# A two-block transformer forward pass: the last retention pair's norm kept on chip, scales stored as rows, and the stream's norm moved into attention

## The chip, the cores and the metric

The kernel runs on one core of one Trainium2 chip. The metric is the device time of one execution in microseconds (us). The engines are PE (matrix products), DVE (VectorE), ACT (ScalarE), POOL (GpSimd) and SP (which issues the DMAs); each executes its own queue in order.

## What is computed

The input is a sequence of 1024 tokens with 1024 channels, in float32. A first block of two hybrid layers (convolutions and windowed attention) is followed by a second block of two layers, each with differential attention and retention side by side, and then a gated FFN. Between the blocks stands an RMS norm. Of the second block, what matters here is:

```python
x = first_block(...)                       # ends in rmsnorm(x, final_norm_g)
for l in range(2):
    u = rmsnorm_2(h, attn_norm[l])
    rq, rk, rv, rg, dq, dk, dv = split(u @ w_in[l])
    ret = rmsnorm_2(retention(rq, rk, rv), ret_norm[l])   # 4 heads, norm over 128
    ret = silu(rg) * ret
    dif = rmsnorm_2(diff_attention(dq, dk, dv, lam), diff_norm[l]) * (1 - lam_init)
    h = h + concat([ret, dif]) @ w_out[l]
    u = rmsnorm_2(h, ffn_norm[l])
    h = h + (silu(u @ w_gate[l]) * (u @ w_up[l])) @ w_down[l]
return rmsnorm_2(h, final_norm)
```

## The kernel before, in words

Everything lies with channels on the 128 partitions and tokens along the free axis, in halves of 512 columns. A float32 product is made of three matmuls on operands split into a rounded high part and a rest (`split`, L189 and L190): high by high, high by low, low by high (L222, L224, L225 in `dense`). Weights are loaded by `load_w` (L202 on SP), their high part is cast on ACT (L205) and the rest is made on POOL (L194).

`second(l, last)` is one layer of the second block. It runs four heads of differential attention (`diff`), then two pairs of retention heads (`retention`, c = 0 and 1), while the projections of the next head and the gates are worked in between. Each finished group of query columns (256 in `diff`, 512 in `retention`) goes through `headnorm`: ACT copies it out of PSUM (L874), SP stores it to DRAM (L875), ACT squares it (L877). One group later, `put_off` has PE sum the columns (`colsum`, L258; DVE L261 takes the mean), POOL takes the power -1/2 (`rsq`, L267) and SP stores the scales to DRAM (L881), one element per descriptor, since tokens lie on the partitions there. The last group of a layer is done by `last_headnorm` (L888).

Later `normed_op` makes an operand of each head: `fetch` loads the head back (L898) and its row of scales, spread over all partitions (L899); DVE multiplies the two and the gain (L1036); for a retention head POOL multiplies the gate (L1038), which was spilled by `gate_spill` and is loaded in halves (L1034); then `split` (L189, L190). In layer 0 the residual stream `xd` still lacks the norm between the blocks: it is loaded (L1070), scaled by a gain on ACT (L1075) and multiplied with the row `R1` (L1064) on POOL (L1077).

The output projection is in two parts. `dense` takes the four differential heads' operands and adds the result to the stream (L1082); this is worked in between the retention of the second pair. `dense_half` takes the four retention heads' operands, for all eight output tiles of the first 512 tokens and then for the other 512 (L1135, L1137, L1138 in `block`), and its result (L1100) feeds the FFN.

The order of all instructions on each queue is planned when the kernel is built: the program is traced, earlier traced work has the higher priority, and an instruction may be put ahead of earlier work that isn't ready in the plan. Buffers come from pools with fixed counts (`xp` has 13 of 8 KB per partition, `dp` six of 2 KB, PSUM's `pt` two banks). `issue_after` keeps a store behind a given one in SP's queue.

The broadcast of a row of scales from tokens on partitions to all partitions is `bcast`: two DVE casts (L275, L276), and per 128 tokens two matmuls on an identity (L282).

Of the kernel before, what the change touches and what calls it, by code (L numbers as in the profile page):

```python
# [20 lines left out]
AF = mybir.ActivationFunctionType  # L21
ALU = mybir.AluOpType
AX = mybir.AxisListType

P = 128
S = 1024
D = 1024
KC = D // P
HW = 512
NT = S // P  # L30
# [28 lines left out]
C_FN1 = C_SINK + 8  # L59
C_AN2 = C_FN1 + 8  # L60
C_RN = C_AN2 + 16
# [4 lines left out]


NTAP0, NTAP = 3, 2
NGATE = 4
RM = 2  # L70
CPW = 256

# [1 line left out]
class Builder:  # L74
    def __init__(self, nc, tc, a, es):
        self.nc, self.tc, self.a, self.es = nc, tc, a, es
        self.n = 0
        self.pools = {}
        self.put_off = None
        self.ready, self.use_ready = [], False  # L80
        self.open(es, cp=1, rp=1, wp=3, xp=13, dp=6, sp=8)
        self.open(es, bass.MemoryType.PSUM, pa=3, ps=2, pt=2, po=1)
        self.open(es, bass.MemoryType.DRAM, dr=2)
# [781 lines left out]
            nc.scalar.copy(c, ps)  # L865
            nc.sync.dma_start(self.R1[:, t], c)

    def headnorm(self, O, n, y, t):

        nc = self.nc
        o = self.tl("ho", (P, HW))
        nc.scalar.copy(o[:, :n], O[:, :n])  # L874
        stored = nc.sync.dma_start(y[0][:, t], o[:, :n])  # L875
        q = self.tl("hq", (P, HW))
        nc.scalar.activation(q[:, :n], o[:, :n], AF.Square)  # L877
        if self.put_off is not None:
            r, rd = self.put_off()
            with self.tc.issue_after(stored.ins):  # L880
                nc.sync.dma_start(rd, r)  # L881
        self.put_off = lambda: (self.rsq(self.colsum([q[:, :n]], P)),
                                y[1][t.start // P:t.stop // P, :].rearrange("c p -> p c"))

    def last_headnorm(self):
        r, rd = self.put_off()
        self.put_off = None
        self.nc.sync.dma_start(rd, r)  # L888

    def nspill(self):  # L890

        return self.yspill(), self.tl("dr", (NT, P), tag="r", bufs=8)

    def fetch(self, y):

# [6 lines left out]
    def ret_units(self, w, c):  # L902
        return [self.proj(w, u) for u in (c, 2 + c, 4 + 2 * c, 5 + 2 * c)]

    def retention(self, l, c, units):
        nc = self.nc
        ys = []
        qf, kf = units[:2]
        ops = self.halves(kf, qf)
        Vs = [self.v_wide(units[2 + j]) for j in range(2)]  # L910
        for j in range(2):
            h = 2 * c + j
            V = Vs[j]
            dec = self.tl("tb", (P, S))
            nc.sync.dma_start(dec, self.a["c_dec"][h])
            y = self.nspill()
            for g in range(2):
                O = self.psT() if g else self.psO()
                nk = 4 * g + 4
                for kt in range(nk):  # L920
                    q0 = max(kt * P, g * HW)
                    n = (g + 1) * HW - q0
                    ps = self.psS()
                    self.scores(ps[:, :n], ops, j, slice(kt * P, kt * P + P), slice(q0, q0 + n))
                    p = self.tl("p", (P, HW))
                    nc.vector.tensor_tensor(p[:, :n], ps[:, :n],
                                            dec[:, q0 - kt * P:q0 - kt * P + n], ALU.mult)
                    pt = self.tl("tp", (P, HW), F32R), self.tl("tp", (P, HW), F32R)
                    nc.scalar.copy(pt[0][:, :n], p[:, :n])
                    if kt % RM:  # L930
                        nc.vector.tensor_tensor(pt[1][:, :n], p[:, :n], pt[0][:, :n].bitcast(F32),
                                                ALU.subtract)
                    else:
                        self.rest(pt[1][:, :n], p[:, :n], pt[0][:, :n])
                    for i, (lhsT, part) in enumerate(V(kt)):
                        nc.tensor.matmul(O[:, HW - n:HW], lhsT, pt[part][:, :n],
                                         start=(kt == 0 and i == 0),
                                         stop=(kt == nk - 1 and i == 2), skip_group_check=True)
                self.headnorm(O, HW, y, slice(g * HW, (g + 1) * HW))
            ys.append(y)  # L940
        return ys

# [3 lines left out]
    def diff(self, l, h, units):  # L946
# [54 lines left out]
            self.headnorm(O, 256, y, slice(g * 256, (g + 1) * 256))  # L1001
        return y

    def gate_spill(self, w, u):
        g = self.tl("dr", (P, S), tag="gate", bufs=4)

        def ev(t, ps):
            self.nc.sync.dma_start(g[:, t], self.silu2(ps, t))

        self.dense(w[u], self.x, ev)  # L1010
        return g
# [30 lines left out]
    def second(self, l, last):  # L1042
        import contextlib
        nc, a = self.nc, self.a
        w, wo = a["w_in_2"][l], a["w_out_2"][l]
        with contextlib.ExitStack() as es:
            self.open(es, pj=4, p=7, tp=6, kl=1, tb=2, ho=2, hq=3)
            self.open_klo()
            yd, gates = [], []
            units = self.diff_units(w, 0)  # L1050
            for h in range(4):
                yd.append(self.diff(l, h, units))
                units = self.diff_units(w, h + 1) if h < 3 else self.ret_units(w, 0)
                if h < NGATE:
                    gates.append(self.gate_spill(w, 8 + h))
            yr = self.retention(l, 0, units)
            units = self.ret_units(w, 1)
            yr += self.retention(l, 1, units)
            gates += [self.gate_spill(w, 8 + h) for h in range(NGATE, 4)]
            self.last_headnorm()  # L1060
            R1 = None
            if l == 0:
                R1 = self.tl("xp", (P, S))
                nc.sync.dma_start(R1, self.R1)  # L1064
            ops = [self.normed_op(yd[h], self.gdn[:, l:l + 1], self.xg) for h in range(4)]
            xs = []
            for d in range(0, KC, 2):
                two = self.tl("xp", (P, 2, S))
                for i in range(2):
                    nc.sync.dma_start(two[:, i, :], self.xd[d + i])  # L1070
                    xs.append(two[:, i, :])
            if l == 0:
                for d in range(KC):
                    for t in (slice(0, HW), slice(HW, S)):
                        nc.scalar.activation(xs[d][:, t], xs[d][:, t], AF.Copy,  # L1075
                                             scale=self.col(C_FN1 + d))
                        nc.gpsimd.tensor_tensor(xs[d][:, t], xs[d][:, t], R1[:, t], ALU.mult)  # L1077
            for d in range(KC):
                xr = xs[d]

                def ev(t, ps):
                    nc.vector.tensor_tensor(xr[:, t], ps, xr[:, t], ALU.add)  # L1082

                self.dense(wo[d][:, 0:4, :], ops, ev)
            ops = [self.normed_op(yr[h], self.col(C_RN + l), self.opt, gates[h]) for h in range(4)]
            es.close()
            self.open(es, fx=6, sw=SW, p1=LEAD)
            xd = [self.tl("dr", (P, S), tag=f"x{d}") for d in range(KC)]
            R = self.R = self.tl("rp", (P, S), tag="R")
            X, q, s1 = {}, [], [None, None]  # L1090
            full = slice(0, HW)
            scale = lambda h: self.row_scale(R, slice(h * HW, (h + 1) * HW), s1[h])
            for h in range(2):
                t = slice(h * HW, (h + 1) * HW)
                s1[h] = self.d2()
                for d in range(KC):
                    xr = xs[d]

                    def ev(t, ps):
                        nc.vector.tensor_tensor(xr[:, t], ps, xr[:, t], ALU.add)  # L1100
                        nc.sync.dma_start(xd[d][:, t], xr[:, t])
                        self.addsq(s1[h], full, xr[:, t], d == 0, eng=1)
                        nc.scalar.activation(xr[:, t], xr[:, t], AF.Copy,
                                             scale=self.col(C_FFN + 8 * l + d))

                    self.dense_half(wo[d][:, 4:8, :], ops, t, ev)
                    self.early_blocks(X, xs, q, h, d)
                    if h == 1 and d == 3:
                        scale(0)
            self.xd = xd  # L1110
            hd, ahead = self.ffn_hidden(a["w_gate_2"][l], a["w_up_2"][l], X,
                                        lambda: scale(1), self.late_blocks(X, xs))
            es.close()
            self.open(es, hx=7, wr=2, sw=1)
            self.ffn_out(l, hd, last, ahead)
# [615 lines left out]
```

## Time and profile before

| what | value |
|---|---|
| median of 3 runs (lowest to highest) | 3629.62 us (3627.13 to 3630.72) |
| the profiled execution's own time | 3628.38 us |
| its span, first to last instruction | 3626.6 us |
| PE busy | 3379.9 us, 93% |
| DVE, ACT, POOL busy | 2509.6, 1565.7, 2096.2 us |
| mean granted PE clock | 0.974 |

Times inside the span are counted from its start. Attention of layer 0 of the second block lies at about 1080 to 1420 us, its hand-over to the FFN at 1420 to 1565; layer 1's hand-over lies at 2700 to 2828. A wait is idle time of an engine just before an instruction, put down to what ended it ("<-"). PEld is PE's weight load, which overlaps the matmuls.

### The profile page before, as it was taken

The numbers are of one execution on the slowest core, as the hardware profiler recorded it, in microseconds if no ns is written. First come the engines' busy times: TensorE is split into PE (matmuls) and PEld (weight loads), VectorE is DVE, ScalarE is ACT, GpSimd is POOL, SyncE is SP. The second block draws the span as 40 slices with busy tenths as digits, with TensorE's granted clock in tenths as the row PEclk, the third lists the DMA queues.
The fourth block names the chain that finished last, engine by engine and source line by source line (L and its number), as shares of the span: only waits on it lengthen the run. The fifth ranks groups of instructions, "written<-read, shape, count | busy, mean of one in ns | idle before, by whom it ended". The sixth has DMA issues, their size and how long they took to land.

```text
span 3626.6 us, 46124 instructions
## 1 busy us (share of the span) xinstructions
PE 3379.9 (93%) x15872; PEld 2777.8 (77%) x15872; DVE 2509.6 (69%) x3947; ACT 1565.7 (43%) x3175; POOL 2096.2 (58%) x1859
## 2 busy tenths in 40 slices
PE   8999999899999999869999989999998789998897
PEld 6788888788888888657777767888886677777676
DVE  6756656655656765667776799766656677767997
ACT  4475442674444553353333333445443533333333
POOL 4785453984472334646666778623334566666784
PEclk9999999999999999989999999999998999999999
DMA  4112532122432335542111243323355422112432
GB/s 129 39 57 54 180 112 74 35 59 82 161 108 53 51 57 111 141 135 89 70 70 72 86 146 111 104 55 53 52 98 148 142 81 79 70 70 82 151 99 82
DMA packets 181451, 330.39 MB, mean 91 GB/s; under 512 B 48992, under 2 KB 59616, under 8 KB 181216
## 3 DMA queue, kind: packets, MB, share of 16 engines
q1 hardware_dynamic: 181216, 327.44, 31.8%
q8 instruction: 125, 2.05, 0.3%
q14 instruction: 110, 0.90, 0.1%
HBM read 250.23 MB, written 73.99 MB: 89 GB/s over the span
## 4 chain that ended last, share of the span: by engine, by line
PE 48%; DVE 10%; DMA 5%; POOL 3%; issue 3%; ACT 1%; SPq 0%; DVEq 0%; POOLq 0%; ACTq 0%
PE pa L222 5%; PE pa L225 5%; PE pa L224 5%; PE pa L1135 3%; PE pa L1137 3%; PE pa L1138 3%; PE T L1138 3%; PE T L1135 2%; PE T L1137 2%; PE ps L1135 2%; PE ps L1138 2%; PE ps L1137 2%; PE po L427 2%; DVE xp L1360 1%; PE ps L334 1%
## 5 line engine op out<-in xcount | busy, mean ns | idle before, releaser
L224 PE MATMUL pa<-xp,whi 128*128 128x512 f32 x2048 | 815.8, 398 | 10.7 <-DVE xp L190 10.7
L222 PE MATMUL pa<-xp,whi 128*128 128x512 f32 x2048 | 813.2, 398 | 11.8 <-ACT xp L189 8.3
L225 PE MATMUL pa<-xp,wlo 128*128 128x512 f32 x2048 | 814.4, 398 | 1.2 <-POOL wlo L194 1.2
L194 POOL TENSOR_TENSOR wlo<-raw,whi 128x512 fp32r<-128x512 f32 x304 | 432.2, 1423 | 468.0 <-ACT whi L205 445.8
L194 POOL TENSOR_TENSOR wlo<-xp,whi 128x512 fp32r<-128x512 f32 x248 | 360.3, 1456 | 192.3 <-ACT whi L1211 191.8
L224 PEld LDWEIGHTS pa<-xp,whi 128*128 128x128 f32 x2048 | 390.1, 190 | 89.9 <-DVE xp L190 16.1
L222 PEld LDWEIGHTS pa<-xp,whi 128*128 128x128 f32 x2048 | 389.8, 191 | 88.1 <-ACT xp L189 9.0
L225 PEld LDWEIGHTS pa<-xp,wlo 128*128 128x128 f32 x2048 | 390.3, 191 | 76.3 <-POOL wlo L194 2.0
L1135 PE MATMUL pa<-xp,whi 128*128 128x512 f32 x672 | 271.3, 405 | 66.8 <-ACT xp L189 22.3
L1211 ACT CAST whi<-xp 128x512 fp32r<-128x512 f32 x248 | 153.8, 620 | 408.1 <-PE T L1137 139.0
L205 ACT CAST whi<-raw 128x512 fp32r<-128x512 f32 x304 | 187.0, 615 | 267.6 <-PE pa L224 145.5
L446 POOL TENSOR_SCALAR p<-p,st 128x256 f32<-128x256 f32 (+4 forms) x224 | 158.1, 714 | 242.9 <-DVE st L985 120.8
L1138 PE MATMUL pa<-xp,wlo 128*128 128x512 f32 x672 | 265.5, 398 | 3.0 <-POOL wlo L194 2.9
L1137 PE MATMUL pa<-xp,whi 128*128 128x512 f32 x672 | 267.2, 398 | 0.0
L701 POOL TENSOR_TENSOR cc<-cc,prod 128x256 f32<-128x256 f32 x240 | 201.0, 859 | 30.0 <-ACT prod L700 23.8
L1135 PEld LDWEIGHTS pa<-xp,whi 128*128 128x128 f32 x672 | 129.0, 192 | 108.1 <-ACT xp L189 22.7
L420 DVE TENSOR_TENSOR tp<-T,tp 128x512 fp32r<-128x512 f32 (+2 forms) x224 | 131.4, 599 | 73.5 <-ACT tp L419 71.7
L980 ACT ACTIVATE p<-p,st 128x384 f32<-128x384 f32 (+3 forms) x192 | 117.1, 611 | 126.4 <-DVE st L973 125.8
L427 PE MATMUL po<-tp,xp 128*128 128x256 f32 (+1 forms) x1024 | 163.6, 279 | 5.1 <-ACT tp L419 4.8
L427 PEld LDWEIGHTS po<-tp,xp 128*128 128x128 f32 x1024 | 148.5, 189 | 24.3 <-ACT tp L419 8.7
L700 ACT ACTIVATE prod<-cc,c 128x256 f32<-128x256 f32 x240 | 119.0, 507 | 109.0 <-POOL cc L701 97.5
L1230 POOL TENSOR_TENSOR xp<-xp,R 128x512 f32<-128x512 f32 x80 | 111.1, 1389 | 84.5 <-DVE xp L1229 84.5
(316 smaller groups left out, 8129.2 us busy)
## 6 DMA issues: line engine op xcount, KB each, us to landing
raw<-w_in SPq DMA_DIRECT2D x208, 256.0 KB, 2.8
xp<-x SPq DMA_DIRECT2D x48, 512.0 KB, 7.3
xp<-w_gate SPq DMA_DIRECT2D x44, 512.0 KB, 5.4
xp<-w_up SPq DMA_DIRECT2D x44, 512.0 KB, 5.2
raw<-w_out SPq DMA_DIRECT2D x80, 256.0 KB, 3.1
x<-xp SPq DMA_DIRECT2D x80, 256.0 KB, 2.1
h<-xp SPq DMA_DIRECT2D x40, 512.0 KB, 3.0
xp<-h SPq DMA_DIRECT2D x80, 256.0 KB, 4.5
```

The costliest lines, as they stand in the source:

```text
L194: self.last_rest = self.nc.gpsimd.tensor_tensor(lo, src, hi.bitcast(F32), ALU.subtract)
L205: nc.scalar.copy(hi, raw)
L222: nc.tensor.matmul(ps[h], hi[:, k - k0, :], x[:, 0, t], start=(k == 0), stop=False)
L224: nc.tensor.matmul(ps[h], hi[:, k - k0, :], x[:, 1, t], start=False, stop=False)
L225: nc.tensor.matmul(ps[h], lo[:, k - k0, :], x[:, 0, t], start=False, stop=(k == nk - 1))
L427: nc.tensor.matmul(O[:, qs[0] * P:qs[0] * P + w], lhsT, pt[part][:, o:o + w], start=((kt, qs) == blocks[0] and i == 0), stop=((kt, qs) == ...
L446: self.nc.gpsimd.tensor_scalar(out, src, colm, 1.0, ALU.mult, ALU.mult)
L701: nc.gpsimd.tensor_tensor(acc[:, i:i + CPW], acc[:, i:i + CPW], q, ALU.add)
L1135: nc.tensor.matmul(ps, hi[:, k, :], xh, start=(start and k == 0), stop=False, skip_group_check=True)
L1137: nc.tensor.matmul(ps, hi[:, k, :], xl, start=False, stop=False, skip_group_check=True)
L1138: nc.tensor.matmul(ps, lo[:, k, :], xh, start=False, stop=(k == len(ops) - 1), skip_group_check=True)
L1211: self.nc.scalar.copy(hi, src)
```

## The change

The last retention pair of each layer isn't spilled any more: `retention` gets the gates, and a `taker` multiplies each group with its broadcast scales (read from PSUM), the gain and the gate, and splits it into an operand. The work that a group leaves behind is a generator in `chains`, which each later `headnorm` advances by one step. The other heads' scales are collected in one tile of 128 by 8, transposed on PE and stored as eight rows, once per head. In layer 0 `scale_stream` norms two tiles of the stream per differential head, from DRAM to DRAM, during attention.

```diff
-    def headnorm(self, O, n, y, t):
+    def headnorm(self, O, n, y, t, take=None):
         o = self.tl("ho", (P, HW))
         nc.scalar.copy(o[:, :n], O[:, :n])
-        stored = nc.sync.dma_start(y[0][:, t], o[:, :n])
+        stored = None
+        if take is None:
+            stored = nc.sync.dma_start(y[0][:, t], o[:, :n])
         q = self.tl("hq", (P, HW))
         nc.scalar.activation(q[:, :n], o[:, :n], AF.Square)
-        if self.put_off is not None:
-            r, rd = self.put_off()
-            with self.tc.issue_after(stored.ins):
-                nc.sync.dma_start(rd, r)
-        self.put_off = lambda: (self.rsq(self.colsum([q[:, :n]], P)),
-                                y[1][t.start // P:t.stop // P, :].rearrange("c p -> p c"))
+        self.advance(stored)
+        self.chains.append(self.spill_scales(q[:, :n], y, t) if take is None else
+                           self.use_scales(q[:, :n], o[:, :n], t, take))
+
+    def advance(self, stored=None):
+        self.stored = stored
+        self.chains = [c for c in self.chains if next(c, 0) is None]
 
     def last_headnorm(self):
-        r, rd = self.put_off()
-        self.put_off = None
-        self.nc.sync.dma_start(rd, r)
+        while self.chains:
+            self.advance()
+
+    def spill_scales(self, q, y, t):
+        nc = self.nc
+        c0, c1 = t.start // P, t.stop // P
+        if c0 == 0:
+            y[2] = self.tl("sp", (P, NT), tag="rt", bufs=3)
+        rt = y[2]
+        m = self.colsum([q], P)
+        nc.gpsimd.tensor_tensor(rt[:, c0:c1], m, self.mhalf[:, c0:c1], ALU.pow)
+        if c1 < NT:
+            return
+        yield
+        ps = self.psT()
+        nc.tensor.transpose(ps[0:NT, 0:P], rt, self.ident)
+        rows = self.tl("sp", (P, P), tag="rows", bufs=2)
+        nc.scalar.copy(rows[0:NT, :], ps[0:NT, 0:P])
+        if self.stored is None:
+            nc.sync.dma_start(y[1], rows[0:NT, :])
+            return
+        yield
...
+        with self.tc.issue_after(self.stored.ins):
+            nc.sync.dma_start(y[1], rows[0:NT, :])
+
+    def use_scales(self, q, o, t, take):
+        r = self.rsq(self.colsum([q], P))
+        yield
+        for _, ps in self.bcast(r):
+            take(o, ps, t)
...
+    def taker(self, o, gcol, g):
+        nc = self.nc
+
+        def take(yy, ps, t):
+            gg = self.d2()
+            nc.sync.dma_start(gg, g[:, t])
+            nc.vector.scalar_tensor_tensor(yy, yy, gcol, ps, ALU.mult, ALU.mult)
+            nc.gpsimd.tensor_tensor(yy, yy, gg, ALU.mult)
+            self.split(o[:, 0, t], o[:, 1, t], yy, 0.5)
+
+        return take
+
+    def retention(self, l, c, units, gates=None):
...
-            y = self.nspill()
+            if gates is None:
+                y, take = self.nspill(), None
+            else:
+                y = self.opt()
+                take = self.taker(y, self.col(C_RN + l), gates[j])
...
+    def scale_stream(self, d):
+        nc = self.nc
+        for h in range(2):
+            t = slice(h * HW, (h + 1) * HW)
+            x, R = self.d2(), self.d2()
+            nc.sync.dma_start(x, self.xd[d][:, t])
+            nc.sync.dma_start(R, self.R1[:, t])
+            nc.scalar.activation(x, x, AF.Copy, scale=self.col(C_FN1 + d))
+            nc.gpsimd.tensor_tensor(x, x, R, ALU.mult)
+            nc.sync.dma_start(self.xd[d][:, t], x)
...
-            self.open(es, pj=4, p=7, tp=6, kl=1, tb=2, ho=2, hq=3)
+            self.open(es, pj=4, p=7, tp=6, kl=1, tb=2, ho=4, hq=3)
...
-                if h < NGATE:
-                    gates.append(self.gate_spill(w, 8 + h))
+                gates.append(self.gate_spill(w, 8 + h))
+                if l == 0:
+                    for d in (2 * h, 2 * h + 1):
+                        self.scale_stream(d)
             yr = self.retention(l, 0, units)
             units = self.ret_units(w, 1)
-            yr += self.retention(l, 1, units)
-            gates += [self.gate_spill(w, 8 + h) for h in range(NGATE, 4)]
+            ops_r = self.retention(l, 1, units, gates[2:])
             self.last_headnorm()
-            R1 = None
-            if l == 0:
-                R1 = self.tl("xp", (P, S))
-                nc.sync.dma_start(R1, self.R1)
...
-            if l == 0:
-                for d in range(KC):
-                    for t in (slice(0, HW), slice(HW, S)):
-                        nc.scalar.activation(xs[d][:, t], xs[d][:, t], AF.Copy,
-                                             scale=self.col(C_FN1 + d))
-                        nc.gpsimd.tensor_tensor(xs[d][:, t], xs[d][:, t], R1[:, t], ALU.mult)
...
-            ops = [self.normed_op(yr[h], self.col(C_RN + l), self.opt, gates[h]) for h in range(4)]
+            ops = [self.normed_op(yr[h], self.col(C_RN + l), self.opt, gates[h]) for h in range(2)]
+            ops += ops_r
```

## Rows read from the trace of the kernel before

**Rows 1.** Windows: stretch, length, busy us of each engine, PE clock, DMA share, GB/s.
```profile
1080.00:1420.00 340.00, 340.00 (x1802) 291.65 (x1800) 223.36 (x501) 161.55 (x369) 111.13 (x116) 1.00 0.32 60
1420.00:1565.00 145.00, 100.69 (x474) 83.67 (x474) 72.38 (x104) 47.57 (x88) 75.38 (x56) 0.86 0.57 129
2700.00:2828.00 128.00, 98.00 (x445) 80.77 (x444) 63.78 (x99) 36.27 (x69) 50.21 (x39) 0.88 0.61 138
```

**Rows 2.** Waits, 1420 to 1640 (layer 0): total us, times, longest us.
```profile
DVE pj L1036 <- DMA pj<-r: 38.1, 4, 20.5
PE pa L1135 <- ACT xp L189: 22.3, 1, 22.3
ACT whi L205 <- DMA raw<-w_out: 21.6, 5, 11.3
PE T L936 <- ACT tp L929: 12.7, 2, 6.7
ACT xp L1075 <- DMA xp<-x: 10.7, 2, 10.4
PE ps L334 <- DVE p L926: 6.2, 1, 6.2
```

**Rows 3.** Waits of PE, 2680 to 2900 (layer 1).
```profile
PE pa L1135 <- DVE xp L1082: 10.2, 1, 10.2
PE T L936 <- DVE tp L931: 9.2, 1, 9.2
PE ps L334 <- DVE p L926: 6.1, 1, 6.1
```

**Rows 4.** Chain that ended last, layer 0's hand-over: start us, us, what.
```profile
1534.49 0.60 ACT ho L874
...
1561.89 1.71 POOL pj L1038
```

**Rows 5.** Timeline of SP's queue, same stretch.
```profile
1546.10 0.39 SPq L888 DMA_DIRECT2D r<-sm  x1
1557.22 0.32 SPq L899 DMA_DIRECT2D pj<-r  x1
```

**Rows 6.** Timeline of PE around layer 0's last wait: start us, busy us.
```profile
1534.80 0.40 PE L1135 MATMUL pa<-xp,whi 128*128 128x512 f32 x1
1535.04 0.39 PE L1137 MATMUL pa<-xp,whi 128*128 128x512 f32 x1
...
1541.65 0.40 PE L1138 MATMUL pa<-xp,wlo 128*128 128x512 f32 x1
1564.31 1.65 PE L1135 MATMUL pa<-xp,whi 128*128 128x512 f32 x3 [22.26 <-ACT xp L189]
...
1568.75 0.63 PE L1137 MATMUL pa<-xp,whi 128*128 128x512 f32 x1
1569.17 0.44 PE L1138 MATMUL pa<-xp,wlo 128*128 128x512 f32 x1
```

**Rows 7.** Chain that ended last, layer 1's hand-over: start us, us, what.
```profile
2768.63 11.61 DMA r<-sm
...
2807.73 12.61 DMA r<-sm
2820.39 4.81 DMA pj<-r
```

**Rows 8.** Lines L282, L1036, L1077: ns min/median/max; what L282's idle ended on.
```profile
L282 PEld LDWEIGHTS T<-identr,sm x160: 185/192/338, 51.0 to 3616.3; 128*128 128x128 f32 x160
...
  DVE sm L275: 15.3, 6
...
L1036 DVE SCALAR_TENSOR_TENSOR pj<-pj,c,pj x32: 736/748/1824, 1440.3 to 2826.0; 128x512 f32<-128x512 f32 x32
L1077 POOL TENSOR_TENSOR xp<-xp,xp x16: 1267/1302/1749, 1471.9 to 1497.6; 128x512 f32<-128x512 f32 x16
```

**Rows 9.** Groups of instructions, 1080 to 1400: busy us, mean ns, idle before.
```profile
L205 ACT CAST whi<-raw 128x512 fp32r<-128x512 f32 x40 | 24.7, 618 | 45.9 <-PE pa L224 19.7 <-issue 11.1 <-DMA raw<-w_in 10.2
```

More of the change, by code (lines that the diff above doesn't have):

```diff
@@ L68 @@
 NTAP0, NTAP = 3, 2
-NGATE = 4
 RM = 2
@@ L78, in __init__ @@
         self.pools = {}
-        self.put_off = None
+        self.chains = []
         self.ready, self.use_ready = [], False
@@ L885, in last_headnorm @@
-    def last_headnorm(self):
-        r, rd = self.put_off()
-        self.put_off = None
-        self.nc.sync.dma_start(rd, r)
+        self.advance(stored)
[4 more added lines that the diff above has]
+        self.chains = [c for c in self.chains if next(c, 0) is None]
+    def last_headnorm(self):
+        while self.chains:
+            self.advance()
@@ new lines, in spill_scales @@
+    def spill_scales(self, q, y, t):
[17 more added lines that the diff above has]
+        yield
+        if self.stored is None:
+            nc.sync.dma_start(y[1], rows[0:NT, :])
+            return
+        with self.tc.issue_after(self.stored.ins):
+            nc.sync.dma_start(y[1], rows[0:NT, :])
@@ L890, in nspill @@
+    def use_scales(self, q, o, t, take):
[3 more added lines that the diff above has]
+            take(o, ps, t)
     def nspill(self):
-        return self.yspill(), self.tl("dr", (NT, P), tag="r", bufs=8)
+        return [self.yspill(), self.tl("dr", (NT, P), tag="r", bufs=8), None]
     def fetch(self, y):
@@ L903, in ret_units @@
         return [self.proj(w, u) for u in (c, 2 + c, 4 + 2 * c, 5 + 2 * c)]
-    def retention(self, l, c, units):
+    def taker(self, o, gcol, g):
[8 more added lines that the diff above has]
+    def retention(self, l, c, units, gates=None):
         nc = self.nc
@@ L938, in retention @@
                                          stop=(kt == nk - 1 and i == 2), skip_group_check=True)
-                self.headnorm(O, HW, y, slice(g * HW, (g + 1) * HW))
+                self.headnorm(O, HW, y, slice(g * HW, (g + 1) * HW), take)
             ys.append(y)
```

## The prediction

> **What bounds the kernel now.** I read the windows first, then who waited for whom, then the chain of work and single queues. In the attention of a layer (340 us of the first one) PE is busy all the time at full clock, while DVE, ACT and POOL have room [rows 1]. There only work added to PE costs time for certain. In the stretch where attention hands over to the first half of the FFN, PE is busy 100.69 us of 145 in layer 0 and 98.00 of 128 in layer 1, and the granted clock averages 0.86 and 0.88 [rows 1]. So 44.3 and 30.0 us of PE idleness stand there, and this is where the change acts.
>
> The waits say what PE waited for. In layer 0: 22.3 us on the last operand's high part (L189), 12.7 in two pieces (6.7 the longest) on ACT's cast of a retention block, 6.2 on a DVE multiply [rows 2]. In layer 1: 10.2, 9.2 and 6.1 [rows 3]. Behind these stand queues held by DMAs: DVE stood 38.1 us at L1036 for the row of scales, ACT 10.7 us at L1075 for the stream and 21.6 us for weights [rows 2].
>
> The last wait in order: ACT copies the last retention block at 1534.49, and the gate multiply of its second use starts only at 1561.89 [rows 4], 27.4 us later. Between them SP issues the store of the scales at 1546.10 and can issue their reload at 1557.22, 11 us on [rows 5]. PE had by then taken `dense_half`'s products as far as the first three heads allow (1534.80 to 1541.65) and stood until 1564.31; after that it ran at the lower of its two levels until 1569.17, a matmul every 0.43 us where full clock gives 0.23 [rows 6]. These 4.9 us cost 4.9 x (1 - 0.23/0.43) = 2.3 us, and I put 2 us on every idle stretch over 6 us: four in layer 0, three in layer 1, 14 in all (an estimate from that one). Layer 1 shows the same round trip: store of scales 12.61 us, reload 4.81; and in its middle another store of 11.61 us in front of the reload that DVE waits for [rows 7].
>
> **The change part by part.**
>
> *The last pair stays on chip.* The stores of y and scales and 4 of the 16 reloads of a layer go (the gate's loads stay). In their place each half of each head has column sum, power, two small DVE casts, eight broadcast matmuls, one DVE multiply reading PSUM, the gate multiply on POOL and a split. All but the matmuls and the casts were there before, later. The DVE multiply with a PSUM operand is not in the trace; between nothing added and the longest L1036, 1.8 us, I take L1036's median 0.75 [rows 8], that is, no change. The chain is then about ten instructions of 0.2 to 1.8 us, some 12 us (an estimate) in place of 27.4. And less of it is exposed: the first 96 matmuls of `dense_half` read only the first halves of all operands, and these need only the block that leaves retention one group earlier. At 0.23 us each [rows 6] that is 22 us of cover for the last group's 12 us. So both end waits go: 22.3 + 10.2 = 32.5 us, and 4 us of clock. **Plus 36.5.** If the cover is gone (the planner puts the chain late), 12 us of chain stand against 6.9 us of other PE work [rows 6], and 5 us per layer come back.
>
> *What it adds on PE.* Eight chains (2 heads, 2 halves, 2 layers) of eight broadcast matmuls. One weight load for them is 0.192 us, the longest 0.338 [rows 8]: 64 x 0.192 = 12.3 us, at most 21.6. PE executes in order, so what stands behind a broadcast waits as well when POOL's power or DVE's casts are late, and that is the dense output projection, for which ACT and POOL prepare the weights; each set also holds one of the two T banks of PSUM while a retention block may hold the other. The broadcasts of before show 15.3 us of such waits in 20 sets (160 matmuls), the six that waited 2.6 us each [rows 8]. Eight sets then cost 6 us at the mean and 20 at the bad rate; I take 12, since these sit between busy queues. Twelve transposes for the stored rows cost at most a broadcast's load each, 2 us. **Minus 26.**
>
> *Scales stored as rows.* Of 48 scattered stores (24 a layer) 8 go with the pair, and 40 become twelve of eight rows of 512 B, each one or two groups later than now. Nobody but the reload waits for them. The scattered form takes 11.61 and 12.61 us [rows 7]; the row form has no row in the trace, and lies between the 4.81 us of the far larger reload and nothing saved. I take the lower end, because it is a simple transfer of 4 KB. With that the 9.2 us in layer 1 goes (store and reload led straight to it [rows 3, 7]), and with it its 2 us of clock. I also count the 6.7 us in layer 0, whose cause is a weight load late behind such a store (ACT's 11.3 us [rows 2]), plus 2. **Plus 20.** The 6.2 and 6.1 us at the start, where DVE waits for the first reloads of the differential heads [rows 2, 3], I count by half with their clock: these reloads stay and only their neighbours shrink. **Plus 8.**
>
> *The stream's norm moves into attention.* Out of the hand-over go 16 ACT scales, 16 POOL multiplies of 1.3 us [rows 8], and the load of R1; the x loads stay. ACT no longer stands 10.7 us at L1075 [rows 2], which held the cast that PE waited 6.0 us for. But in layer 1, without this norm, there is still idleness in the middle, so I count half: **plus 4.** In attention it adds, for 16 halves, two loads and one store (48 issues on SP, 12.6 MB), an ACT scale and a POOL multiply. POOL would go from 111 to 132 us of 340 [rows 1], ACT by some 10. PE's full queue hides both, and I cost them at nothing. The cover is the lead of the weight loads. Each store waits on SP for its POOL multiply, and queued behind it are weight loads, y stores and gate stores; ACT's weight cast waits for these.
>
> Sum: 36.5 - 26 + 20 + 8 + 4 = 42.5 us. The profiled execution has 3628.4 us, 1.8 over its span, and lies 1.2 under the median of 3629.6, so 3628.4 - 42.5 = 3585.9 becomes **3587** as a median.
>
> **The rivals.**
>
> *All waits go.* Against the forecast's half counts: 44.3 + 30.0 idle and 14 of clock, less 14 of added PE work and no new waits: 74 us, **3555**. For it speaks that DVE, ACT and POOL are each busy under 60% of these stretches [rows 1]; against it, that the reloads of four differential heads and of 4 MB of x remain in the same 30 us. Chance 0.14.
>
> *The middle waits stay, in another dress.* The order is planned at build time and every queue is in order, so DVE or ACT stops at another late load. The on-chip operands also hold two more of the 13 large buffers: four for retention, four for differential operands, four for the stream and these two are 14, and the last stream tile has to wait for a value tile. Then only the ends count: 36.5 - 26 = 10.5, **3619**. It also covers the case that the change doesn't do what it says because the planner puts the new chains late. Chance 0.18, a little under half of it within 0.2%.
>
> *SP holds up attention.* This one ends slower. If a scaled half's store sits at SP's head while its loads, scale and multiply finish (4.8 us for a large load [rows 7], 0.6 for an ACT pass [rows 4], 1.3), the weight load behind it is late by 7 us less its lead. PE has no idleness there to absorb it. It decides from 42.5/16 = 2.7 us per half; at 4 us, 64 us are lost and the time is **3651**. For it: the weight buffers are two, so a load's lead is short, and POOL, which frees them, gets the new multiplies. Against it: before 40 weight casts ACT waited only 10.2 us in all for a load [rows 9], and PE was never idle. Chance 0.13.
>
> *POOL slows DVE in attention.* The rows show DVE's L1036 at 0.736 to 1.824 us for one shape, and POOL's L1077 at 1.267 to 1.749 [rows 8]: when both run, one instruction takes up to 1.08 us longer. Sixteen multiplies moved beside DVE's score work cost it at most 16 x 1.08 = 17 us, and PE would lose them if DVE were its next limit: **3604**. DVE is idle a third of that stage [rows 1], so the chance is 0.05. The Trainium skill ("GPSIMD Engine Reference", Key points) says that GpSimd shares its SBUF interfaces with VectorE and contends with DVE instructions that have two SBUF inputs; it speaks against this move. By that rule, the spread in these rows agrees, but no row here says which partner an instruction ran against.
>
> **How the numbers follow.** A measurement of this kernel can tell about 0.2%, 7.3 us, from no change. The forecast (3569 to 3607 by its own terms: the halves taken whole with 6 us of new waits, or not at all with 20) has 0.50. Faster by over 0.2%: 0.50 + 0.14 + 0.05 and 0.10 of the second rival, 0.79. Within: 0.08 of that rival and 0.02 of SP's, 0.10. Slower: 0.11. The range runs from 3560, which leaves out half of "all waits go" (0.07), to 3627, which leaves out SP's case (0.13).
>
> **What would show it.** Right: no store or reload of scales between the last retention block and `dense_half`; PE's idle stretches of 22.3 and 10.2 us gone and the clock full there; broadcast matmuls inside the retention stretch with waits under 2 us each; the scale stores landing in a few us; L1077's work inside attention with PE still full. Wrong: PE idle in attention behind weight casts, or the idleness of 6 us each at the first reloads unchanged, or PE standing at broadcasts for more than 20 us in all.

## Result, and the profile after

The changed kernel takes 3587.22 us (median of 4 runs, 3581.94 to 3589.81), the kernel before on the same chip 3628.38 (4 runs, 3624.82 to 3630.72): ratio 0.9885, 95% interval 0.9873 to 0.9898, that is 41 us less. The forecast was 3587, inside 3560 to 3627. The sum was right; the experiments show that its two largest terms were not.

The changed kernel's page, packets:

```profile
DMA packets 168956, 336.16 MB, mean 94 GB/s; under 512 B 32432, under 2 KB 43152, under 8 KB 168720
```

The bytes rose by 6 MB, while packets under 512 B, of which the kernel before has 48992, fell by a third.

Its windows, columns as in [rows 1]: layer 0's attention, then layer 0's hand-over cut into four.

```profile
1080.00:1420.00 340.00, 340.00 (x1798) 291.25 (x1797) 229.21 (x497) 173.21 (x388) 131.83 (x132) 1.00 0.30 98
1420.00:1480.00 60.00, 53.92 (x302) 45.76 (x301) 44.91 (x88) 31.15 (x62) 32.55 (x28) 0.96 0.32 100
1480.00:1540.00 60.00, 55.89 (x234) 45.85 (x234) 26.66 (x37) 13.88 (x23) 22.23 (x16) 0.93 0.45 162
1540.00:1600.00 60.00, 55.46 (x236) 43.38 (x235) 53.12 (x62) 39.54 (x69) 37.94 (x25) 0.94 0.53 174
1600.00:1660.00 60.00, 47.22 (x178) 37.20 (x179) 45.12 (x50) 18.09 (x33) 35.34 (x24) 0.83 0.23 71
```

Attention has taken the stream's norm: POOL 131.83 us where 111.13 were [rows 1], ACT 173.21 where 161.55 were, and PE is still full. In the hand-over the idleness has shrunk, but at 1600 to 1660, where the FFN begins, 12.8 us of it stand and the granted clock is 0.83.

PE's longest waits of the changed kernel at the same place, 1400 to 1640 (waiting line, what it waited for, total us, times, longest):

```profile
PE T L281 <- DVE sm L274: 5.4, 2, 4.9
PE pa L221 <- DVE xp L1138: 4.1, 1, 4.1
PE T L281 <- DVE sm L275: 2.9, 1, 2.9
PE pa L1192 <- DVE xp L1237: 2.6, 1, 2.6
PE pa L1192 <- ACT whi L204: 2.5, 1, 2.5
```

The 22.3, the 12.7 and the 6.2 us of [rows 2] are all gone. What is left are small waits. The longest, at the broadcast line L281, is not one of the pair's new broadcasts; by its time it belongs to the row of scales for the FFN, which the kernel before broadcasts as well:

```profile
1608.01 0.44 PE L281 MATMUL T<-identr,sm 128*128 128x128 f32 x1 [4.90 <-DVE sm L274]
```

In layer 1, likewise, nothing of the 10.2, 9.2 and 6.1 us of [rows 3] is left; the longest there is 4.8.

A landmark shows where the time was won. The FFN's multiply of the stream (L1230 of the kernel before, L1287 of the changed one) occurs 80 times; the view of the line gives min/median/max ns, then first and last start. Before:

```profile
L1230 POOL TENSOR_TENSOR xp<-xp,R x80: 1269/1296/1683, 1647.4 to 3339.1; 128x512 f32<-128x512 f32 x80
```

After:

```profile
L1287 POOL TENSOR_TENSOR xp<-xp,R x80: 1282/1296/1687, 1623.0 to 3299.0; 128x512 f32<-128x512 f32 x80
```

24.4 us are won by the FFN of layer 0, 40.1 by the last multiply of layer 1. At the first weight loads of layer 1's retention, just ahead of its hand-over, the lead is still 22.4 us (first starts, before and after):

```profile
L936 PEld LDWEIGHTS T<-tp,xp x96: 186/188/333, 2677.7 to 2799.5; 128*128 128x128 f32 x96
L989 PEld LDWEIGHTS T<-tp,xp x96: 186/188/335, 2655.3 to 2728.1; 128*128 128x128 f32 x96
```

So the gain lies in the two hand-overs.

### The profile page after: what moved, and what is told of

The parts are those of the page before. It is cut to its first block, busy times and chain, and to the rows that moved or that the text cites. A ratio compares the mean times of both kernels' runs of the same rounds, so it can differ in the third digit from the quotient of the medians.

```text
span 3586.4 us, 46309 instructions
## 1 busy us (share of the span) xinstructions
PE 3390.6 (95%) x15948; PEld 2785.1 (78%) x15948; DVE 2508.4 (70%) x3963; ACT 1570.2 (44%) x3187; POOL 2088.5 (58%) x1859
## 4 chain that ended last, share of the span: by engine, by line
PE 70%; DVE 13%; POOL 8%; issue 4%; ACT 2%; DMA 2%; SPq 0%; DVEq 0%; POOLq 0%; ACTq 0%
PE pa L221 11%; PE pa L223 11%; PE pa L224 11%; PE pa L1195 3%; PE pa L1192 3%; PE pa L1194 3%; PE po L426 3%; POOL wlo L193 3%; PE T L1195 3%; PE T L1192 2%; PE T L1194 2%; POOL cc L700 2%; PE T L415 2%; PE ps L333 2%; PE ps L334 2%
## 5 line engine op out<-in xcount | busy, mean ns | idle before, releaser
L1287 POOL TENSOR_TENSOR xp<-xp,R 128x512 f32<-128x512 f32 x80 | 111.3, 1391 | 86.0 <-DVE xp L1286 86.0
```

## Experiments

The change has three parts: the pair kept on chip, the scales stored as rows, and the stream's norm in attention. Each was undone alone, and each made alone. All ratios are to the kernel before, run on the same chip (medians 3618.86, 3617.7 and 3621.57 us for the three sets); 0.1% is 3.6 us. The times in the expectations count from the 3628 us of the first chip, so they are compared here as ratios. Differences in us are taken from the ratios, unless they are called medians. Diffs are against the changed kernel.

All of these kernels but the two with gate tiles (below) also keep four tiles for copies of a finished block (`ho`), where the kernel before has two. That is not what the rows are worth: with the pair spilled, two such tiles (and gate tiles of their own) give 0.9823, four give 0.9811.

### One part undone

**The pair spilled again** (rows and stream's norm stay):

```diff
-            ops_r = self.retention(l, 1, units, gates[2:])
+            yr += self.retention(l, 1, units)
...
-                   gates[h]) for h in range(2)]
-            ops += ops_r
+                   gates[h]) for h in range(4)]
```

> The changed kernel with the last retention pair spilled again (its scales as rows too). By the terms of the prediction the pair on chip is worth 36.5 - 26 = 10.5 us, somewhat less once the store is quick: 3592 to 3600. Rival, the pair carries nearly the whole gain and rows and stream only come along: 3615 to 3628. Either way PE should again stand before the first dense_half products that need the fourth head, for 10 us or more in layer 0.

Measured: 0.9813 (0.9796 to 0.9829), 3550.83 us. Without its first-named part the change is worth 68 us and not 41. Both ranges missed it, and so did the wait of 10 us or more that was expected either way: PE's longest waits there, in layer 0 and layer 1, are

```profile
PE T L281 <- DVE sm L274: 6.0, 2, 4.5
PE T L281 <- DVE sm L274: 5.8, 2, 4.5
```

The same kernel beside the changed one in a later set (below) gave 0.9811.

**Scattered stores of the scales** (pair and stream's norm stay):

```diff
-        m = self.colsum([q], P)
-        nc.gpsimd.tensor_tensor(rt[:, c0:c1], m, self.mhalf[:, c0:c1], ALU.pow)
...
-            nc.sync.dma_start(y[1], rows[0:NT, :])
+        r = self.rsq(self.colsum([q], P))
+        nc.sync.dma_start(y[1][c0:c1, :].rearrange("c p -> p c"), r)
```

> The changed kernel with the remaining scales stored scattered again, one group later, as before. By the terms the rows are worth 20 us and part of the 8 at the first reloads: 3607 to 3615. Rival, scattered stores cost nothing once no store stands in front of the last wait: 3585 to 3592.

Measured: 0.9995 (0.9985 to 1.0004). Without the rows the other two parts together are worth nothing, which is less than both expectations.

**The stream's norm back in the hand-over** (pair and rows stay):

```diff
-                if l == 0:
-                    for d in (2 * h, 2 * h + 1):
-                        self.scale_stream(d)
...
+            if l == 0:
+                for d in range(KC):
+                    for t in (slice(0, HW), slice(HW, S)):
+                        nc.scalar.activation(xs[d][:, t], xs[d][:, t], AF.Copy,
+                                             scale=self.col(C_FN1 + d))
+                        nc.gpsimd.tensor_tensor(xs[d][:, t], xs[d][:, t], R1[:, t], ALU.mult)
```

> The changed kernel with the norm of the stream back in the hand-over (layer 0). By the terms 4 us: 3589 to 3595. Rival, the 21 us of POOL and the large buffer for R1 hold the hand-over now that it is dense: 3600 to 3615.

Measured: 0.992 (0.9905 to 0.9935), at the border of the two ranges (0.9908 and 0.9922). Beside the other two, the moved norm is worth 0.35% against the first measurement of the changed kernel, 0.15% against its later one (0.9905, below). Its window of attention:

```profile
1080.00:1420.00 340.00, 340.00 (x1807) 291.59 (x1805) 221.59 (x500) 162.40 (x372) 110.79 (x116) 1.00 0.18 60
```

With the norm in attention DVE is busy 229.21 us, without it 221.59, though none of the moved work is DVE's. One group of DVE's instructions, first without and then with the norm in attention, carries the largest part of these 7.6 us:

```profile
L1042 DVE SCALAR_TENSOR_TENSOR p<-p,st,p 128x512 f32<-128x512 f32 x16 | 14.1, 895 | 1.9 <-POOL p L445 1.9
L1042 DVE SCALAR_TENSOR_TENSOR p<-p,st,p 128x512 f32<-128x512 f32 x16 | 18.5, 1173 | 3.2 <-POOL p L445 3.2
```

It takes two large operands from tiles in SBUF, while DVE's multiply of PSUM by a row (L230) keeps its 686 and 685 ns. POOL's 16 multiplies are the likely cause; no run moves them without ACT's scales and the DMAs. PE is full both times.

### One part alone

The edits are the same, two undone at a time.

> The kernel before with the last pair kept on chip alone (scattered stores for the others, stream's norm in the hand-over). By the terms of the prediction 10.5 us: 3615 to 3621. Rival, the pair carries nearly the whole gain: 3587 to 3600.

Only the pair: 0.9952 (0.9935 to 0.9969), 17 us faster (11 to 24 by the interval; the medians differ by 14.5). That is above the forecast's 10.5, whose range (0.9963 to 0.998) the interval touches, and outside the rival's.

> The kernel before with the scales stored as rows alone. By the terms 20 to 28 us: 3600 to 3610, and the last wait of each layer shorter by the 9 us that store and reload lose. Rival, rows alone leave the last wait as it is, since three steps now stand between the block and the store: 3620 to 3632.

Only the rows: 0.9845 (0.983 to 0.9859), 56 us faster, more than the whole change and twice what was expected. Its windows (attention; layer 0's hand-over; layer 1's):

```profile
1080.00:1420.00 340.00, 340.00 (x1802) 291.40 (x1800) 222.49 (x501) 163.13 (x373) 110.57 (x116) 1.00 0.18 60
1420.00:1660.00 240.00, 208.93 (x937) 167.56 (x936) 178.26 (x224) 112.89 (x203) 151.64 (x110) 0.94 0.42 144
2640.00:2900.00 260.00, 239.75 (x1097) 192.38 (x1096) 194.31 (x254) 120.06 (x215) 145.42 (x106) 0.97 0.40 138
```

and the longest wait of PE in its first hand-over:

```profile
PE pa L1198 <- ACT xp L188: 8.7, 1, 8.7
```

The DMA engines are busy 18% of attention where the kernel before had 32% at the same 60 GB/s [rows 1]. The last operand is still spilled and reloaded here, and yet the wait for it falls from 22.3 us [rows 2] to 8.7, and in layer 1, where it was 10.2 [rows 3], PE waits nowhere longer than 4.1 us. Two things did this. The first is the store itself. The chain that ended last, in this kernel's first hand-over, has store and reload as (start us, us):

```profile
1521.25 1.20 DMA r<-rows
1522.52 3.74 DMA pj<-r
```

The store took 11.61 and 12.61 us in [rows 7], and reload followed store by 11.1 us in [rows 5]. The way from ACT's copy of the last block to the gate multiply, 27.4 us before [rows 4], is 13.6 here:

```profile
1513.54 0.57 ACT L872 COPY ho<-T 128x512 f32<-128x512 f32 x1
1527.18 2.93 POOL L1103 TENSOR_TENSOR pj<-pj,dp 128x512 f32<-128x512 f32 x2 [7.27 <-DVE pj L1101]
```

Some 10 of the 13.8 us saved are the store. The edit also makes 16 stores of 48 and moves their times, so the rest isn't traced to one of these.

The second is that PE has other work to do meanwhile. In the kernel with rows, stream's norm and spilled pair (the first experiment) the same way still takes 19.8 us in layer 0, and yet PE is busy for all of it. The copy, the multiply and the window between them, then the window of [rows 4] in the kernel before:

```profile
1499.88 0.58 ACT L872 COPY ho<-T 128x512 f32<-128x512 f32 x1
1519.68 2.99 POOL L1103 TENSOR_TENSOR pj<-pj,dp 128x512 f32<-128x512 f32 x2 [0.63 <-DVE pj L1101]
1499.88:1519.68 19.80, 19.80 (x93) 16.40 (x92) 4.93 (x9) 3.33 (x7) 6.12 (x6) 1.00 0.34 111
...
1534.49:1561.89 27.40, 7.56 (x37) 6.01 (x36) 1.68 (x4) 1.64 (x3) 2.30 (x2) 0.70 0.23 68
```

Of its 93 matmuls 72 are dense products of the differential heads, of which the kernel before had 2 left in that window. In layer 1 the way is 18.7 us in the same kernel, again with PE busy throughout. So the end wait was in part the form of the store; for the rest the round trip stays, and is hidden.

> The kernel before with the stream's norm moved into attention alone. By the terms 4 us: 3622 to 3628, with PE still full in attention of layer 0. Rival, SP holds up attention: slower, 3635 to 3655.

Only the stream's norm: 1.0022 (1.0012 to 1.0031), 8 us slower: the rival's direction, at the lowest end of its range. In its attention PE is no longer full:

```profile
1080.00:1420.00 340.00, 330.11 (x1728) 282.49 (x1727) 218.34 (x485) 165.99 (x373) 125.64 (x127) 0.98 0.42 96
```

and its waits there, PE's longest and ACT's for the stream's tiles, are:

```profile
PE po L426 <- ACT tp L418: 8.8, 2, 4.5
...
ACT dp L1053 <- DMA dp<-x: 36.3, 12, 11.2
```

ACT stands up to 11.2 us at its scale of the stream (L1053), whose load is late (these loads take 2.6 to 12.3 us to land), and PE then waits for ACT. With the rows beside it (the first experiment, which differs in the form of the stores alone) PE is busy 340.00 of 340 there, and in the changed kernel the same wait of ACT is 13.6 us in all and 3.1 at the longest. The kernel with pair and stream's norm but scattered stores shows the same (PE busy 328.33 of 340). So the moved norm needs the rows.

### What the pair costs

Given the rows, the pair costs 27 us (changed kernel without the stream's norm against rows alone: 0.992 and 0.9845), and 26 to 37 beside both (0.9813 against the changed kernel's first measurement, medians of the repeats below). Three suspects: the broadcast matmuls, DVE's work at the entry of the FFN, and SP's queue.

**Each broadcast of the pair made twice**, the first set of results unread:

```diff
         yield
+        for _ in self.bcast(r):
+            pass
         for _, ps in self.bcast(r):
             take(o, ps, t)
```

> The changed kernel with every broadcast of the pair's scales made twice (the first one unread): eight more sets of eight matmuls and two casts. By the prediction PE is full there, so a set costs its 1.5 us and up to as much again in waits: plus 12 to 24 us, 3599 to 3611. Rival, the hand-over has room that the FFN's entry swallows anyway: plus 0 to 6 us, 3587 to 3593.

Measured: 0.9926 (0.9911 to 0.994). Against the two measurements of the changed kernel (0.9885, 0.9905) that is 15 or 8 us for 64 more matmuls; the interval of the second (0.9882 to 0.9927) overlaps. A price about that of the forecast's 12.3 us of PE time fits, but is not settled. The rival's 0 to 6 us isn't excluded either.

**The squares of the FFN's norm added on POOL in place of DVE**, because DVE is busy 30.00 of 30 us at 1580 to 1610 while PE is busy 17.87:

```diff
-self.addsq(s1[h], full, xr[:, t], d == 0, eng=1)
+self.addsq(s1[h], full, xr[:, t], d == 0, eng=0)
```

> The changed kernel with the sums of squares of the second output projection added on POOL instead of DVE (14 instructions of about 1 us a layer). In the trace of after DVE is busy without a gap at the FFN's entry while PE falls idle. If DVE bounds that entry, it takes 5 to 20 us off: 3567 to 3582. Rival, POOL is the next limit there, since it makes the weights' low parts: 3585 to 3600.

Measured: 0.9906 (0.9889 to 0.9922), in the rival's range. DVE is still busy 29.90 of those 30 us, and no time is won that can be told from the changed kernel. These additions are not what holds the entry up; whether DVE's other work or POOL does was not tried.

**SP's queue.** Four kernels on one chip: tiles of their own for the pair's gates, so that they no longer take those of the spilled retention heads' gates (and two `ho` tiles instead of four, to make room); the changed kernel again; the spilled pair again; and the spilled pair with such tiles for all gates of the reloads, as a control.

```diff
-            self.open(es, pj=4, p=7, tp=6, kl=1, tb=2, ho=4, hq=3)
+            self.open(es, pj=4, p=7, tp=6, kl=1, tb=2, ho=2, hq=3, gt=4)
...
-            gg = self.d2()
+            gg = self.tl("gt", (P, HW))
             nc.sync.dma_start(gg, g[:, t])
```

> The changed kernel with four tiles of their own for the gates of the pair on chip (and two instead of four copies of a finished block, to make room). In the trace of after SP stands 15.5 and 20.7 us in the hand-overs on a gate load of a spilled head, until the pair's POOL multiply frees one of the six small tiles, with the reload of the last differential head and all loads of the stream queued behind it. If that is why the pair on chip costs some 27 us beside the rows, the stream's loads come some 20 us (layer 0) and 40 us (layer 1) sooner and most of the 27 us comes back: ratio to before 0.980 to 0.984. Rivals: the two large buffers that the pair holds make the loads late, or the broadcasts fill PE: then it stays at the changed kernel's ratio, 0.987 to 0.991.

> The changed kernel itself, on the same chip as the others of this call, for pairs: ratio to before as measured first, 0.987 to 0.991. It also prices the doubled broadcasts of the earlier run (0.9926).

> The spilled pair with rows and the norm of the stream in attention once more, beside the gate tiles: 0.980 to 0.983. If the gate tiles undo the pair's only cost, the two agree within 0.3%; if broadcasts cost PE too, this one stays faster by 8 us or more.

> The spilled pair (rows, stream in attention) with four tiles of their own for all gates at reload. SP waits only 4.3 us for such a tile there, so by the theory it changes little: within 0.3% of the spilled pair. Rival: gates loaded sooner free SP before the last waits, another 5 to 10 us.

| kernel | us | ratio to before (95%) |
|---|---|---|
| changed kernel again | 3589.78 | 0.9905 (0.9882 to 0.9927) |
| pair's gates with own tiles | 3577.81 | 0.9881 (0.9866 to 0.9896) |
| pair spilled again | 3552.64 | 0.9811 (0.9796 to 0.9825) |
| pair spilled, gates with own tiles | 3555.5 | 0.9823 (0.9809 to 0.9838) |

On this chip the pair costs 37 us by the medians (34 by the ratios). The tiles give back 12 by the medians and 9 by the ratios, but the two intervals overlap, and the changed kernel's first measurement (0.9885) leaves 1; so their gain is not shown. It is in any case not most of the cost, as was expected, and without the pair they give nothing. The expectations for the repeats and the control came. What the tiles remove, in SP's waits of the changed kernel at 1400 to 1500:

```profile
SPq L1099 <- POOL ho L948: 15.5, 2, 9.0
```

This is the gate load of a spilled retention head. Its pool has six tiles, and the pair's gates hold them until POOL has multiplied (L948), so SP stands 15.5 us (20.7 in layer 1) with the next reloads of scales and the loads of the stream queued behind it. With own tiles this wait is gone, but SP stands at the next load instead:

```profile
SPq L934 <- DVE xp L189: 24.7, 2, 23.9
```

So the stream's loads come hardly earlier. First and last start of these 16 loads, in the changed kernel as it was first measured:

```profile
L1132 SPq DMA_DIRECT2D xp<-x x16: 319/514/750, 1481.1 to 2743.5; - x16
```

with the pair's own gate tiles:

```profile
L1132 SPq DMA_DIRECT2D xp<-x x16: 320/446/1052, 1480.0 to 2741.3; - x16
```

and with the pair spilled:

```profile
L1132 SPq DMA_DIRECT2D xp<-x x16: 320/514/1263, 1457.0 to 2695.5; - x16
```

24 us earlier without the pair in layer 0, and 48 by the last of layer 1, the lead gained in layer 0 among them. The wait at L934 is for a `pj` tile that frees only when the splits of the differential operands have read it. ACT's timeline shows when these ran. With own gate tiles:

```profile
1474.45 0.63 ACT L188 ACTIVATE xp<-ho 128x512 fp32r<-128x512 f32 x1 [1.90 <-POOL ho L948]
1474.98 3.22 ACT L188 ACTIVATE xp<-pj 128x512 fp32r<-128x512 f32 x6
```

With the pair spilled:

```profile
1440.62 1.16 ACT L188 ACTIVATE xp<-pj 128x512 fp32r<-128x512 f32 x2
...
1445.94 1.30 ACT L188 ACTIVATE xp<-pj 128x512 fp32r<-128x512 f32 x2 [0.54 <-DVE pj L1101]
```

In the planned order ACT splits the differential operands (xp<-pj) only behind the first split of the pair's second operand (xp<-ho, which waits for POOL); six of them were ready and run back to back at 1474.98. With the pair spilled they start at 1440.62, 34 us earlier. This fits what PE does there: dense products run while retention ends, as in the window of 19.8 us above. In that kernel PE is busy, same windows as above:

```profile
1420.00:1660.00 240.00, 219.43 (x977) 176.08 (x976) 180.26 (x232) 107.18 (x194) 139.43 (x99) 0.95 0.42 142
2640.00:2900.00 260.00, 240.43 (x1082) 192.66 (x1081) 193.35 (x250) 117.66 (x212) 147.73 (x107) 0.96 0.39 134
```

The changed kernel has 212.49 and 233.89 us there, 6.1 of them in each layer the added broadcasts (32 x 0.192). So it does some 13 us less of other work per layer, 26 in both, which is most of the pair's cost; fixed stretches of two kernels that run apart give this only as an estimate.

What remains open: whether the differential operands come late because the pair's second operand takes one of the 13 large buffers ahead of them, or because the planner simply orders ACT's work so. A kernel with the differential operands made first, or with separate buffers, was not tried. Nor is the split of the cost between this order, the gate tiles and the broadcasts settled.

The best kernel measured is the change without its pair: 3551 and 3553 us, 1.9% under the kernel before and 0.7 to 1.0% under the changed one.

## Why the prediction was right, and where it was not

**"The last pair stays on chip", plus 36.5 and minus 26.** The end waits went, as forecast, and the pair alone is worth 17 us against the 10.5 of these two terms. But the credit was given to the wrong part. The step that failed is the reading of the 27.4 us round trip as one that only keeping the pair on chip removes. The rows alone halve it in layer 0 (13.6 us) and take the wait from 22.3 to 8.7 us; with the stream's norm beside them the round trip is 19.8 us, and PE has enough dense products for all of it, so that it waits nowhere in either hand-over longer than 4.5 us although the pair is spilled. Beside them the pair's 36.5 us are therefore hardly there, and a cost stays: 26 to 37 us where 26 were forecast.

That the forecast's cost comes near is partly luck. Two of its entries hold: L947 takes 0.742 us at the median (0.75 forecast), and the 64 matmuls are there. But the 12 us of waits at them are not. In layer 0 PE stood 1.0 us at the pair's broadcasts, in layer 1 2.3 us. What the view of L281 shows for the stretches 1440 to 1490 and 2690 to 2745, which hold all of them:

```profile
  DVE sm L275: 0.6, 1
  issue: 0.4, 1
...
  PE T L989: 1.1, 1
  DVE sm L274: 1.0, 1
  issue: 0.2, 1
```

The whole line L281 stood 30.0 us on DVE's casts, 10 more than before, but it stands nearly as long with the pair spilled (29.8 us in the first experiment, 25.8 in its repeat), so most of this isn't the pair's. In place of these waits the runs show the late splits of the differential heads and the loads of the stream that come 24 us later. What the forecast missed is "all but the matmuls and the casts were there before, later". The gate loads and splits that moved forward stand in front of other heads' in SP's and ACT's queues; how many us each is worth is open.

**"Scales stored as rows", plus 20, and the first reloads, plus 8.** This is the term that was mis-sized most: alone the rows give 56 us against 28. The row form of the store, put at 4.8 us, took 1.20. The 9.2 and 6.7 us in the middle went, and the waits of 6.2 and 6.1 us at the first reloads, counted by half, went whole. The rest lies at the end waits, less in layer 0 and gone in layer 1. I priced the store by who waited for it, and left out those who waited behind it.

**"The stream's norm", plus 4.** Beside the rows it gives 12 us (rows and norm against rows alone: 0.9813 and 0.9845, on different chips), and 5 to 13 beside rows and pair; alone it costs 8. "PE's full queue hides both, and I cost them at nothing" held in the changed kernel. It fell with the scattered stores.

**The rivals.** *SP holds up attention* is real, but only without the rows, at 10 us (340 less 330.11) and not 64, and at another queue: ACT stood at the stream's late load. SP's waits at the stores of the stream are 15.3 us there and 21.0 in the changed kernel, where PE is full. *POOL slows DVE in attention*: DVE's work grows by 7.6 us where 17 were the bound, most of all in an instruction with two operands in SBUF, and DVE's idle time hides it. By the Trainium skill ("GPSIMD Engine Reference", Key points), GpSimd and VectorE contend for shared SBUF interfaces; this growth of DVE's busy time agrees with it, and the price is below what DVE has to spare here. *All waits go* (74 us) is near what the change gives without the pair (68), which it didn't suppose. *The middle waits stay* did not come; the queues that it names are where the pair's operands stand in front of others, and the buffers were not tested.

**The clock.** Fourteen us were put on clock, and the forecast expected it full after the end waits. It is 0.93 at 1480 to 1540 and 0.83 at 1600 to 1660: PE's idleness has become several short stretches, and the granted clock still falls in them.

**The signs.** Of those for "right", the end waits went, the pair's broadcasts waited at most 1.1 us each, the row store landed in 1.20 us (in the kernel with rows alone), and the stream's norm runs inside attention with PE full. The clock is not full, and reloads of the other heads' scales are still issued behind the last retention block (at 1478.28, 1480.68 and 1490.10, the block's copy starting at 1472.41). Of those for "wrong" none came, if the more than 20 us at broadcasts is read as waits that were added.

So 42.5 us by the sum and 41 measured agree because errors cancel, which is luck. By single edits the three parts alone give 17, 56 and -8 us, 65 together, and the whole gives 41: the parts overlap.

## What to carry to other kernels

Where two edits each claim the same wait, price the cheaper one alone first and give the other only what is left; here storing a few KB as rows was worth more (56 us alone) than the redesign that avoids a part of these stores (17). A store's price is what waits behind it as much as who waits for it. And when an operand is made earlier, list every load and split that it now stands in front of, in each queue and in each pool of tiles.

## What the runs showed of the hardware beyond that

Stores scattered in pieces under 512 B fill the DMA engines far beyond their bytes: in attention, at 60 GB/s, their mean busy share is 0.32 with the scattered form and 0.18 with rows. A scattered store took 7.6 to 13.7 us to land (L881 of the kernel before), the row store in the chain above 1.20. PE's transposes for the rows cost little: twelve matmuls of 0.272 us (L905), and ACT's copies of them 0.254 us each (L907).
